# Chunk-by-chunk products ahead of each norm, a third weight pair and a divided gate chain in a two-block transformer on one core

## The chip, the cores and the metric

The kernel runs on one core of a Trainium2 chip. The metric is the device time of one execution in microseconds, the median of several runs. Three runs of the kernel before took 2664.5, 2668.2 and 2671.23 us.

## What is computed

The reference is a transformer of two blocks on one sequence of 512 tokens of width 1024. The first block has two layers over the tokens and, in layer 0, over 256 context tokens beside them. A layer takes a norm with a shift and a scale from a modulation vector, a wide projection, a mixer (a bidirectional chunkwise mLSTM with gates, a gated unit and a convolution over 31 tokens), an out-projection, a second norm, and a gated FFN of 22 x 128 hidden columns. The second block runs two attentions (A: three groups of dilated windows; B: one window of 128 with shared keys), each with a layer norm and a gate behind it:

```
mod = silu(c) @ w_mod[l] + b_mod[l]           # six vectors: sh1, sc1, g1, sh2, sc2, g2
p = (rmsnorm(x, norm1_g) * (1 + sc1) + sh1) @ w_in
x = x + g1 * (mixer(p) @ w_out)
x = x + g2 * swiglu(rmsnorm(x, norm2_g) * (1 + sc2) + sh2, w_gu, w_down)
# second block, twice
x = layer_norm(ALPHA * x + mixer_i(x))
x = x + sigmoid(x @ ple_w_gate[i]) * (p[i] @ ple_w_proj[i])
```

## The kernel before, in words

Every float32 factor is split into a high and a low part, and a product is three matmuls: high by high, low by high, high by low (`mm`, L138). Activations stand in transposed tiles (`Hh`, `Hl`); tokens go in chunks of 128, `c`: six in layer 0, four in layer 1 and in the second block.

Weights come block by block through `wblock` (L154): two loads of 512 KB into `raw` (three buffers, all issued on SP), then for each half a copy to `hi` on ACT and a subtraction to `lo` on DVE. The pool `wp` has two `hi`/`lo` pairs, so a third block's copies wait until TensorE is done with the first. SP issues its loads in their order: a load that waits for a buffer holds back all behind it.

`wide` (L215) makes the 1024 output columns of a product in two halves `n` of 512; for each it takes the two halves `kh` of the inner dimension in turn, and for each `kh` all chunks. It serves the FFN's down products, the products behind both attentions (`post_attention`) and their gate (`embed_gate`).

The FFN of a layer takes its 22 hidden blocks in groups (`GROUPS`: 8, 8 and 6). For each block it multiplies with `w_gu` and leaves the gated result in `ah` and `al`; behind a group the down products add its share to the residual `xt`: `resid` multiplies with the gate `g2` on DVE (`ot`) and adds on POOL (`w`). Behind the last group each chunk is normed (squares on ACT, a sum and a power on DVE and POOL, two scalings) and, by way of the list `pend`, transposed on TensorE (`finish_T`, L338, or `split_T`, L401) for the next stage. `pend.upto(c)` and `pend.keep(n)` say where in the program these transposes stand.

The modulation vectors are made by generators `mod_gen`: one vector takes four steps, in each a load of 1 MB (two of eight row blocks) into `wm` (one buffer) and its matmuls into the bank `md`, which the sixteen records `md<-wm,cact` in the trace are, and a last step that adds the bias and hands the row on. In layer 0's FFN five vectors are made, 20 loads; in layer 1's one, 4 loads. `modl.pump(n)` takes `n` steps behind each hidden block (3 in layer 0, 1 in layer 1), and `modl.drain()` at the end of the first group takes what is left.

`gates` (L641) makes the mLSTM's decay factors in one chain over all engines, which ends in an activation on ACT and six transposes on TensorE (L738). It stands ahead of the convolution's products.

In attention A, heads go in four quads, in each three groups. A quad's first group copies rotated queries and keys (`qh`, `qr`) to `kh`, `qs`, `ks` and `w`, and values to `vb`, by many small DMAs on SP. The tile framework orders each engine's instructions from the program ahead of time; each engine then runs them in that order.

Of the kernel before, what the change touches and what calls it, by code (L numbers as in the profile page):

```python
# [23 lines left out]
GROUPS = [list(range(0, 8)), list(range(8, 16)), list(range(16, 22))]  # L24
# [46 lines left out]
def emit(ctx, tc, a, out):  # L71
    nc = tc.nc
# [81 lines left out]
    def wblock(src, nk, n, into=None):  # L154
        hi, lo = into or (T(wp, [128, nk, n], t, F32R) for t in ("hi", "lo"))
# [49 lines left out]

    def tmj(lhs, wb, n0, n, ps):
# [8 lines left out]
    def wide(src, nk, lhs, chs, bank, use, pre=None, early=None, first=None):  # L215

        for n in range(2):
            ps = {}
            for kh in range(2):
                hi, lo = ({(0, 0): first, (0, 1): early}.get((n, kh)) or wblock(src[n, kh], nk, 512))  # L220
                for c in chs:
                    if pre:
                        pre(c, n, kh)
                    if kh == 0:
                        ps[c] = bank(c)
                    for k in range(nk):
                        lh, ll = lhs(c, nk * kh + k)
                        mm(ps[c], lh, hi[:, k, :], kh + k == 0, False)
                        mm(ps[c], lh, lo[:, k, :], False, False)
                        mm(ps[c], ll, hi[:, k, :], False, kh == 1 and k == nk - 1)  # L230
                    if kh == 1:
                        use(c, n, ps[c])
# [203 lines left out]
    def projections(l, MIX, H, hook):  # L436
# [41 lines left out]
        gates(l, gt, r, t3)  # L478

        for m in range(2):  # L480
            wb = win(4 + m)
# [3 lines left out]
            hook(1)  # L485
            y = yb[:, m, :]
            for p, (o, n) in zip(fm(wb, 128, H, segs), segs):
                stt(y[:, o:o + n], p, col(C_CA + m), sg[:, o:o + n], ADD, MUL)
            convl.add(conv(m, y, yc[:, m, :], col, last, PJ))
# [151 lines left out]
    def gates(l, gt, r, t3):  # L641
# [7 lines left out]
        ax = T(sm, sh, "ga", bufs=1)  # L649
        act(ax, f, AF.Abs)  # L650
        u = T(sm, sh, "gu", bufs=1)
        act(u, ax, AF.Exp, scale=-1.0)
        w = T(sm, sh, "gw", bufs=1)
        ts(w, u, 1.0, ADD)
        lw = T(sm, sh, "glw", bufs=1)
        act(lw, w, AF.Ln)
        rw = T(sm, sh, "grw", bufs=1)
# [9 lines left out]
        for j in range(6):  # L667
            for d, c in enumerate((FCH[j], BCH[j])):
                G.tensor_copy(gpl[:, j, d, 32 * d:32 * d + 4], lf[:, c, d, :])
                G.tensor_copy(gpi[:, j, d, 32 * d:32 * d + 4], gv[:, c, d, 0, :])  # L670
        pc = trt()
# [1172 lines left out]
```

## Time and profile before

| what | value |
|---|---|
| median of three runs | 2668.2 us (2664.5 to 2671.23) |
| profiled execution | 2671.3 us |
| its span | 2669.2 us |
| TensorE busy | 2578.8 us, 97% |
| mean granted TensorE clock | 0.989 |
| DMA | 314.72 MB, mean 118 GB/s |

The span is the time from the first to the last instruction of the profiled execution; the 2.1 us beside it lie around it. TensorE is busy nearly throughout; what it is not busy for lies in short stretches between stages.

### The profile page before, as it was taken

Reading aid. Unit: us, or ns where it says so; the run is one execution under the profiler, and the core shown is the slowest. Engines: PE = TensorE matmul, PEld = TensorE weight load, DVE = VectorE, ACT = ScalarE, POOL = GpSimd, SP = SyncE. Lnnn points to the kernel's source line nnn. Section 1 sums busy time; section 2 is a strip of 40 time slices with the busy share of each in tenths; the row PEclk is TensorE's granted clock in tenths of the full one; section 3 lists DMA queues with packets and bytes.
Section 4 is the critical chain, followed back from the end, with each engine's and each line's share of the span. In section 5 each row is a group of like instructions: output and inputs, shape, how many; then the busy total and the mean of one; then the engine's idle time right before and its main releaser. Section 6 shows DMA issues by size and latency. Waiting matters only on the chain.

```text
span 2669.2 us, 39682 instructions
## 1 busy us (share of the span) xinstructions
PE 2578.8 (97%) x15360; PEld 2166.1 (81%) x15360; DVE 1310.8 (49%) x2802; ACT 964.3 (36%) x2017; POOL 519.9 (19%) x574
## 2 busy tenths in 40 slices
PE   7999999999999998999999999999999999999998
PEld 5888788778888888887878888788787888778787
DVE  5675655223323335766533333534454444675666
ACT  3423535111221225345422222334344344443753
POOL 1155532002002013034302020411111111021102
PEclk9999999999999999999999999999999999999999
DMA  8311553652112123127433232433434344534442
GB/s 301 123 56 46 180 180 112 213 178 64 64 64 64 60 69 106 65 77 223 137 124 95 95 95 83 133 106 98 137 106 130 116 120 125 161 103 141 120 166 79
DMA packets 129979, 314.72 MB, mean 118 GB/s; under 512 B 18528, under 2 KB 48832, under 8 KB 129792
## 3 DMA queue, kind: packets, MB, share of 16 engines
q1 hardware_dynamic: 129792, 312.20, 36.8%
q8 instruction: 121, 1.98, 0.3%
q14 instruction: 66, 0.54, 0.1%
HBM read 272.02 MB, written 13.89 MB: 107 GB/s over the span
## 4 chain that ended last, share of the span: by engine, by line
PE 79%; DVE 7%; DMA 5%; ACT 3%; POOL 3%; issue 2%; SPq 1%; POOLq 0%; DVEq 0%; ACTq 0%
PE mm L138 67%; PE md L138 5%; PE tr L138 5%; PE tr L1228 1%; DVE lo L124 1%; DVE w L124 1%; SPq L1376 1%; POOL w L124 1%; DMA wm<-in_w_mod_dram 1%; DMA t<-mwd 1%; ACT hi L121 1%; DMA raw<-in_a_in_dram 1%; POOL rs L124 1%; ACT t L121 1%; DVE xs L131 1%
## 5 line engine op out<-in xcount | busy, mean ns | idle before, releaser
L138 PE MATMUL mm<-Hh,hi 128*128 128x512 f32 (+1 forms) x2192 | 797.0, 364 | 6.6 <-ACT hi L121 5.5
L138 PE MATMUL mm<-Hl,hi 128*128 128x512 f32 (+1 forms) x2192 | 768.5, 361 | 0.2 <-DVE Hl L124 0.2
L138 PE MATMUL mm<-Hh,lo 128*128 128x512 f32 (+1 forms) x2192 | 712.1, 362 | 0.0
L121 ACT ACTIVATE hi<-raw 128x1024 fp32r<-128x1024 f32 (+2 forms) x334 | 338.0, 1042 | 836.6 <-PE mm L138 461.6
L124 DVE TENSOR_TENSOR lo<-raw,hi 128x1024 fp32r<-128x1024 f32 (+2 forms) x334 | 422.3, 1286 | 299.2 <-ACT hi L121 298.8
L138 PEld LDWEIGHTS mm<-Hh,hi 128*128 128x128 f32 x2192 | 413.8, 189 | 101.4 <-ACT hi L121 8.1
L138 PEld LDWEIGHTS mm<-Hl,hi 128*128 128x128 f32 x2192 | 413.8, 189 | 66.7 <-issue 0.6
L138 PEld LDWEIGHTS mm<-Hh,lo 128*128 128x128 f32 x2192 | 378.3, 189 | 46.9 <-issue 3.5
L124 POOL TENSOR_TENSOR w<-w,ot 128x256 f32<-128x256 f32 x160 | 127.4, 815 | 909.4 <-DVE ot L124 905.2
L124 DVE TENSOR_TENSOR sg<-mm,sg 128x512 f32<-128x512 f32 (+1 forms) x132 | 75.7, 599 | 406.1 <-PE mm L138 233.2
L138 PE MATMUL mm<-hi,Hh 128*128 128x256 f32 (+2 forms) x740 | 225.7, 306 | 6.5 <-ACT Hh L121 3.3
L138 PE MATMUL mm<-hi,Hl 128*128 128x256 f32 (+2 forms) x740 | 221.5, 300 | 0.5 <-POOL Hl L124 0.5
L138 PE MATMUL mm<-lo,Hh 128*128 128x256 f32 (+2 forms) x740 | 220.8, 299 | 0.0
L124 POOL TENSOR_TENSOR qr<-rt,rt 128x512 f32<-128x512 f32 x58 | 85.5, 1487 | 487.0 <-DVE rt L124 366.9
L138 PEld LDWEIGHTS mm<-hi,Hh 128*128 128x128 f32 x740 | 141.6, 192 | 15.3 <-ACT Hh L121 3.7
L138 PEld LDWEIGHTS mm<-hi,Hl 128*128 128x128 f32 x740 | 141.9, 192 | 6.1 <-issue 1.2
L138 PEld LDWEIGHTS mm<-lo,Hh 128*128 128x128 f32 x740 | 142.2, 192 | 3.7
L138 PE MATMUL mm<-hi,ah 128*128 128x512 f32 x352 | 139.3, 396 | 0.0
L138 PE MATMUL mm<-hi,al 128*128 128x512 f32 x352 | 139.2, 396 | 0.0
L138 PE MATMUL mm<-lo,ah 128*128 128x512 f32 x352 | 139.2, 396 | 0.0
L138 PE MATMUL mm<-hi,Yh 128*128 128x256 f32 (+1 forms) x416 | 130.3, 313 | 5.2 <-DVE t L124 3.1
L124 DVE TENSOR_TENSOR rt<-mm,cs 128x512 f32<-128x512 f32 x116 | 75.5, 685 | 116.6 <-PE mm L138 111.7
(369 smaller groups left out, 3692.8 us busy)
## 6 DMA issues: line engine op xcount, KB each, us to landing
raw<-in_w_gu_dram SPq DMA_DIRECT2D x88, 512.0 KB
raw<-in_a_in_dram SPq DMA_DIRECT2D x72, 512.0 KB
wm<-in_w_mod_dram SPq DMA_DIRECT2D x24, 1024.0 KB
raw<-in_w_in_dram SPq DMA_DIRECT2D x40, 512.0 KB
raw<-in_w_d_dram SPq DMA_DIRECT2D x40, 512.0 KB
raw<-in_w_mod_dram SPq DMA_DIRECT2D x36, 512.0 KB
t<-mwd SPq DMA_DIRECT2D x38, 256.0 KB
raw<-in_w_out_dram SPq DMA_DIRECT2D x16, 512.0 KB
```

The lines of the kernel that those rows point to most:

```text
L121: return S.activation(o, i, f, **kw)
L124: return (e or V).tensor_tensor(out=o, in0=x, in1=y, op=op)
L131: (e or V).tensor_scalar(out=o, in0=x, scalar1=s1, scalar2=None, op0=op0)
L138: lasts["P"] = PE.matmul(o, lhsT=l, rhs=r, start=start, stop=stop, **kw).ins
L1228: PE.transpose(pt[:, 128 * i:128 * i + 128], e, ident)
L1376: ld(d["v"][32 * c:32 * c + 32, b, :], d["vr"][32 * b:32 * b + 32, c, :])
```

## The change

- `GROUPS` becomes 4, 6, 6 and 6 hidden blocks; `ah` and `al` have six buffers in place of eight; the down weights are packed to fit.
- `wblock` has three `hi`/`lo` pairs. The gates' temporaries move into one tile of the convolution's pool, and the DMA scratch is set to 512.
- `wide` loads both `kh` halves of its second half `n` and takes it chunk by chunk (both `kh` for a chunk before the next): in the last FFN group, behind attention and in the gate. The out-projection takes its last two column blocks chunk by chunk.
- `w_gu[0]` (in layer 1 `w_gu[1]` too) is loaded during the out-projection. In layer 1 a new function, `fm_pairs`, takes the first 256 tokens of the first two FFN blocks before the others.
- `gates` becomes a generator whose steps stand between the convolution's products.
- The points at which chunks are transposed move: `pend.keep(1)` in layer 0's last group too, `upto(c + 1)` in `embed_gate`, `upto(1 + j)` at attention A's first products.

```diff
@@ -21,7 +21,7 @@
...
 HID = 22
-GROUPS = [list(range(0, 8)), list(range(8, 16)), list(range(16, 22))]
+GROUPS = [list(range(0, 4)), list(range(4, 10)), list(range(10, 16)), list(range(16, 22))]
 FCH = [4, 5, 0, 1, 2, 3]
@@ -152,7 +152,7 @@
     def wblock(src, nk, n, into=None):
-        hi, lo = into or (T(wp, [128, nk, n], t, F32R) for t in ("hi", "lo"))
+        hi, lo = into or (T(wp, [128, nk, n], t, F32R, bufs=3) for t in ("hi", "lo"))
         h = (nk + 1) // 2
@@ -203,6 +203,16 @@
...
+    def fm_pairs(wbs, H, first):
+        pss = [[[mmt()] for _ in range(2)] for _ in wbs]
+        for q in range(2):
+            for i, wb in enumerate(wbs):
+                pend.upto(first + i if q == 0 else 9)
+                for m in range(2):
+                    fm_into([pss[i][m][0][:, 256 * q:256 * q + 256]], wb, 128 * m, H, [(256 * q, 256)])
+        return pss
     def tmj(lhs, wb, n0, n, ps):
@@ -212,24 +222,30 @@
...
-    def wide(src, nk, lhs, chs, bank, use, pre=None, early=None, first=None):
+    def wide(src, nk, lhs, chs, bank, use, pre=None, early=None, first=None, by_chunk=True):
         for n in range(2):
-            ps = {}
-            for kh in range(2):
-                hi, lo = ({(0, 0): first, (0, 1): early}.get((n, kh)) or wblock(src[n, kh], nk, 512))
-                for c in chs:
-                    if pre:
-                        pre(c, n, kh)
-                    if kh == 0:
-                        ps[c] = bank(c)
-                    for k in range(nk):
-                        lh, ll = lhs(c, nk * kh + k)
-                        mm(ps[c], lh, hi[:, k, :], kh + k == 0, False)
-                        mm(ps[c], lh, lo[:, k, :], False, False)
-                        mm(ps[c], ll, hi[:, k, :], False, kh == 1 and k == nk - 1)
-                    if kh == 1:
-                        use(c, n, ps[c])
+            ps, wb = {}, {}
+            order = [(kh, c) for kh in range(2) for c in chs]
+            if n and by_chunk:
+                wb = {kh: wblock(src[n, kh], nk, 512) for kh in range(2)}
+                order = [(kh, c) for c in chs for kh in range(2)]
+            for kh, c in order:
+                if kh not in wb:
+                    wb[kh] = {(0, 0): first, (0, 1): early}.get((n, kh)) or wblock(src[n, kh], nk, 512)
+                hi, lo = wb[kh]
+                if pre:
+                    pre(c, n, kh)
+                if kh == 0:
+                    ps[c] = bank(c)
+                for k in range(nk):
+                    lh, ll = lhs(c, nk * kh + k)
+                    mm(ps[c], lh, hi[:, k, :], kh + k == 0, False)
+                    mm(ps[c], lh, lo[:, k, :], False, False)
+                    mm(ps[c], ll, hi[:, k, :], False, kh == 1 and k == nk - 1)
+                if kh == 1:
+                    use(c, n, ps[c])
@@ -475,17 +491,22 @@
...
         qT = T(MIX, [128, 4, TT_], "qT")
-        gates(l, gt, r, t3)
-
+        gsteps = gates(l, gt, r, t3, PJ)
+        next(gsteps)
+        wbc = [win(4), win(5)]
         for m in range(2):
-            wb = win(4 + m)
+            wb = wbc[m]
             sg = t3()
...
             hook(1)
+            next(gsteps, None)
             y = yb[:, m, :]
...
                 stt(y[:, o:o + n], p, col(C_CA + m), sg[:, o:o + n], ADD, MUL)
+            if m == 0:
+                next(gsteps)
             convl.add(conv(m, y, yc[:, m, :], col, last, PJ))
@@ -646,15 +667,20 @@
...
         sh = [128, 6, 2, 4]
-        ax = T(sm, sh, "ga", bufs=1)
+        sp = T(PJ, [128, 256], "ct", bufs=1)
+        def small(i):
+            return sp[:, 48 * i:48 * i + 48].rearrange("p (c d h) -> p c d h", c=6, d=2)
+        ax = small(0)
         act(ax, f, AF.Abs)
-        u = T(sm, sh, "gu", bufs=1)
+        u = small(1)
         act(u, ax, AF.Exp, scale=-1.0)
-        w = T(sm, sh, "gw", bufs=1)
+        w = small(2)
         ts(w, u, 1.0, ADD)
-        lw = T(sm, sh, "glw", bufs=1)
+        lw = small(3)
         act(lw, w, AF.Ln)
-        rw = T(sm, sh, "grw", bufs=1)
+        rw = small(4)
         V.reciprocal(out=rw, in_=w)
@@ -668,6 +694,7 @@
...
                 G.tensor_copy(gpi[:, j, d, 32 * d:32 * d + 4], gv[:, c, d, 0, :])
+        yield
         pc = trt()
@@ -708,6 +735,7 @@
...
                     tt(mp[p, j + 1:j + 2], br[p, j, le:le + 1], M[p, j, le:le + 1], ADD)
+        yield
         for d in range(2):
@@ -733,6 +761,7 @@
...
         act(E, E, AF.Exp, scale=-1.0)
+        yield
         pe_ = trt()
@@ -949,11 +978,17 @@
...
         rest = [c for c in chs if c >= ne]
-        for n, cc in ((0, first), (1, first), (0, rest), (1, rest), (2, chs), (3, chs)):
-            if n not in wbo:
-                wbo[n] = wblock(a["w_out"][l, n], 8, 256)
-            wb = wbo[n]
-            for c in cc:
+        gu = {}
+        order = [(n, c) for n, cc in ((0, first), (1, first), (0, rest), (1, rest)) for c in cc]
+        order += [(n, c) for c in chs for n in (2, 3)]
+        for n, c in order:
+                if n not in wbo:
+                    wbo[n] = wblock(a["w_out"][l, n], 8, 256)
+                if (n, c) == (3, chs[-2]):
+                    gu[0] = wblock(a["w_gu"][l, 0], 8, 256)
+                if last and (n, c) == (3, chs[-1]):
+                    gu[1] = wblock(a["w_gu"][l, 1], 8, 256)
+                wb = wbo[n]
                 if n or c >= ne:
@@ -978,12 +1013,20 @@
...
             for jj in grp:
-                with behind("AV" if jj == 1 else ""):
-                    wb = wblock(a["w_gu"][l, jj], 8, 256)
-                ah = T(FP, [128, TT_], "ah", F32R, bufs=8)
-                al = T(FP, [128, TT_], "al", F32R, bufs=8)
-                if jj == 0:
+                if jj in gu:
+                    wb = gu[jj]
+                else:
+                    with behind("AV" if jj == 1 else ""):
+                        wb = wblock(a["w_gu"][l, jj], 8, 256)
+                ah = T(FP, [128, TT_], "ah", F32R, bufs=6)
+                al = T(FP, [128, TT_], "al", F32R, bufs=6)
+                if jj == 0 and last:
+                    both = fm_pairs([wb, gu[1]], H2, 2)
+                    pg, pu = both[0]
+                elif jj == 0:
                     pg, pu = fm_pair(wb, H2, segs)
+                elif jj == 1 and last:
+                    pg, pu = both[1]
                 else:
@@ -1015,7 +1058,7 @@
...
                 if lastg and n2 == 1:
-                    pend.keep(1 if last else 2)
+                    pend.keep(1)
                 for n in (2 * n2, 2 * n2 + 1):
@@ -1025,9 +1068,9 @@
...
-            wide(a["w_d8"][l, gi] if gi < 2 else a["w_d6"][l], len(grp) // 2,
+            wide(a["w_d4"][l] if gi == 0 else a["w_d6"][l, gi - 1], len(grp) // 2,
                  lambda c, k: [t[:, 128 * c:128 * c + 128] for t in acts[grp[k]]], chs,
-                 lambda c: mmt() if c < 4 else (mdt, trt)[c - 4](), down)
+                 lambda c: mmt() if c < 4 else (mdt, trt)[c - 4](), down, by_chunk=lastg)
         close(FP)
@@ -1293,7 +1336,7 @@
...
         def pre(c, n, kh):
-            pend.upto(c + 2)
+            pend.upto(c + 1)
             if (n, kh) == (0, 1):
@@ -1384,7 +1427,7 @@
...
                 for j, (i, m) in enumerate(((0, 0), (0, 1), (1, 0))):
-                    pend.upto(3 if h or j else 2)
+                    pend.upto(3 if h else 1 + j)
                     half = lambda z: from_residue(z)[:, 2 * h:2 * h + 2]
@@ -1830,7 +1874,7 @@
...
-    nc = bacc.Bacc("TRN2", target_bir_lowering=False, num_devices=1)
+    nc = bacc.Bacc("TRN2", target_bir_lowering=False, num_devices=1, dynamic_dma_scratch_size=512)
     arrays, args = {}, {}
```

What moves, first on TensorE in layer 0's FFN, at the last modulation pieces (`md<-wm,cact`, one row for a piece; `mm<-hi,ah` and the like are down products). Before, the last piece of all and its surroundings:

```order
L138 MATMUL mm_5952<-hi_5903,ah_4999 128x512
L138 MATMUL mm_5952<-lo_5904,ah_4999 128x512
L138 MATMUL mm_5952<-hi_5903,al_5000 128x512
L138 MATMUL mm_5952<-hi_5903,ah_5150 128x512
L138 MATMUL md_5718<-wm_5873,cact 32x256 x8
L138 MATMUL mm_5952<-lo_5904,ah_5150 128x512
L138 MATMUL mm_5952<-hi_5903,al_5151 128x512
L138 MATMUL mm_5913<-hi_5991,ah_5300 128x512
```

The change, from the twelfth of the twenty pieces on:

```order
L138 MATMUL mm_5580<-hi_5549,al_4593 128x512
L138 MATMUL md_5253<-wm_5296,cact 32x256 x8
L138 MATMUL mm_5580<-hi_5549,ah_4846 128x512
L138 MATMUL mm_5580<-lo_5550,ah_4846 128x512
L138 MATMUL mm_5580<-hi_5549,al_4847 128x512
L299 MATMUL tr_5308<-ident,mb_5254 128x128 x2
L138 MATMUL md_5312<-wm_5315,cact 32x256 x8
L138 MATMUL md_5312<-wm_5325,cact 32x256 x8
L138 MATMUL md_5312<-wm_5335,cact 32x256 x8
L138 MATMUL md_5312<-wm_5345,cact 32x256 x8
L138 MATMUL md_5360<-wm_5364,cact 32x256 x8
L138 MATMUL md_5360<-wm_5374,cact 32x256 x8
```

Before, at least 23 products lie ahead of every piece; in the change the last eight pieces stand in a row, two more of them behind the last row shown, and three products and two transposes ahead of them.

Next on TensorE in layer 1, where the gates' chain ends (`tr<-ident,w` are the six transposes; `mm_9603`, `mm_9645`, and in the change `mm_9690`, `mm_9747` and `mm_9792` are the convolution's inputs). Before:

```order
L138 MATMUL mm_9603<-Hh_8425,lo_9567 128x512
L138 MATMUL mm_9645<-Hh_8425,hi_9634 128x512
L138 MATMUL mm_9645<-Hl_8426,hi_9634 128x512
L738 MATMUL tr_9552<-ident,w_9549 128x36 x6
L138 MATMUL mm_9645<-Hh_8425,lo_9635 128x512
L138 MATMUL mm_9645<-Hh_8425,hi_9634 128x512
L138 MATMUL mm_9645<-Hl_8426,hi_9634 128x512
```

The change:

```order
L138 MATMUL mm_9747<-Hh_8545,lo_9583 128x512
L138 MATMUL mm_9747<-Hh_8545,hi_9582 128x512
L138 MATMUL mm_9747<-Hl_8546,hi_9582 128x512
L138 MATMUL mm_9747<-Hh_8545,lo_9583 128x512
L767 MATMUL tr_9778<-ident,w_9738 128x36 x6
L138 MATMUL mm_9792<-Hh_8545,hi_9582 128x512
L138 MATMUL mm_9792<-Hl_8546,hi_9582 128x512
L138 MATMUL mm_9792<-Hh_8545,lo_9583 128x512
```

Before, the transposes stand behind two matmuls of the second product; in the change behind all 24 of it.

Last on SP at the first boundary between quads of attention A (`raw` are weights, `kh`, `qs` and `ks` the copies of the quad's first group). Before:

```order
L159 DMA raw_16041<-in_a_in_dram 128x1024
L159 DMA raw_16045<-in_a_in_dram 128x1024
L159 DMA raw_16231<-in_a_in_dram 128x1024
L1171 DMA kh_15837<-qh_15848 32x512 x8
L1171 DMA qs_15835<-qr_15846 32x512 x4
L1171 DMA ks_15836<-qr_15846 32x512 x4
L1171 DMA kh_15837<-qh_15869 32x512 x8
L1171 DMA qs_15835<-qr_15867 32x512 x4
L1171 DMA ks_15836<-qr_15867 32x512 x4
```

The change:

```order
L159 DMA raw_16305<-in_a_in_dram 128x1024
L159 DMA raw_16491<-in_a_in_dram 128x1024
L159 DMA raw_16495<-in_a_in_dram 128x1024
L159 DMA raw_16651<-in_a_in_dram 128x1024
L1214 DMA kh_16097<-qh_16108 32x512 x8
L1214 DMA qs_16095<-qr_16106 32x512 x4
L1214 DMA ks_16096<-qr_16106 32x512 x4
```

Before, one half (`raw_16231`) of the blocks that follow the first group stands ahead of the copies (the two loads ahead of it are the values' weights), and the next half behind the sixteen `vb` copies; in the change three stand ahead (from `raw_16491` on), and the fourth behind `vb` and the next block's `qs` copies.

## Rows read from the trace of the kernel before

**Rows 1.** The page's busy time by engine.

```profile
PE 2578.8 (97%) x15360; PEld 2166.1 (81%) x15360; DVE 1310.8 (49%) x2802; ACT 964.3 (36%) x2017; POOL 519.9 (19%) x574
```

**Rows 2.** Stretches: width, PE busy (instructions), granted clock, DMA share, GB/s.

```profile
440.00:600.00 160.00, 159.19 (x1092) 1.00 0.57 196
110.00:126.00 16.00, 14.09 (x76) 0.89 0.03 6
996.00:1030.00 34.00, 25.30 (x151) 0.95 0.50 164
1070.00:1090.00 20.00, 16.18 (x65) 0.83 0.18 57
1300.00:1320.00 20.00, 16.16 (x121) 0.91 0.17 58
1680.00:1716.00 36.00, 29.92 (x177) 0.91 0.43 147
1876.00:1900.00 24.00, 19.38 (x122) 0.93 0.47 141
2016.00:2040.00 24.00, 19.01 (x125) 1.00 0.44 137
2156.00:2180.00 24.00, 20.16 (x125) 0.93 0.46 137
2306.00:2390.00 84.00, 80.26 (x352) 0.98 0.38 120
2608.00:2648.00 40.00, 37.24 (x170) 0.96 0.11 36
```

**Rows 3.** Waits, 1070 to 1090: engine, line, releaser; us, times, longest.

```profile
PE tr L738 <- ACT w L121: 3.8, 1, 3.8
```

**Rows 4.** Waits of PE in layer 0's FFN, 440 to 600.

```profile
PE md L138 <- DMA wm<-in_w_mod_dram: 0.6, 3, 0.2
```

**Rows 5.** The chain that ended last, layer 0's FFN: start, us, what.

```profile
485.18 5.30 DMA wm<-in_w_mod_dram
...
490.52 1.07 PE md L138 x16
491.59 5.55 PE mm L138 x31
```

**Rows 6.** The same chain, a run of down products.

```profile
620.85 11.24 PE mm L138 x48
```

**Rows 7.** Waits of PE at the first quad boundary, 1876 to 1900.

```profile
PE mm L138 <- ACT hi L121: 2.2, 1, 2.2
PE tr L1228 <- ACT sb L121: 1.0, 2, 0.8
```

**Rows 8.** Timeline of SP ahead of that boundary: start, us, what was issued.

```profile
1831.12 1.76 SPq L159 DMA_DIRECT2D raw<-in_a_in_dram  x2
1843.76 4.97 SPq L1171 DMA_DIRECT2D kh<-qh  x8
...
1877.94 10.05 SPq L1376 DMA_DIRECT2D vb<-vr  x16
1888.04 11.14 SPq L159 DMA_DIRECT2D raw<-in_a_in_dram  x6
```

**Rows 9.** Timeline at the end of layer 1's FFN, one chunk's norm chain.

```profile
1684.34 0.76 DVE L124 TENSOR_TENSOR ot<-mm,g 128x256 f32<-128x256 f32 x2 [6.77 <-PE mm L138]
...
1689.13 0.66 PE L401 MATMUL tr<-ident,w 128*128 128x128 f32 x4 [0.70 <-DVE w L127]
...
1690.26 0.66 PE L401 MATMUL tr<-ident,w 128*128 128x128 f32 x4 [0.47 <-POOL w L124]
```

**Rows 10.** The page's groups of instructions: the residual adds on POOL.

```profile
L124 POOL TENSOR_TENSOR w<-w,ot 128x256 f32<-128x256 f32 x160 | 127.4, 815 | 909.4 <-DVE ot L124 905.2
```

**Rows 11.** The page's DMA queues: packets, MB, share of 16 engines.

```profile
q1 hardware_dynamic: 129792, 312.20, 36.8%
```

More of the change, by code (lines that the diff above doesn't have):

```diff
@@ L639, in conv_post, with gates @@
                 tt(o, o, sg[:, 256 * m:256 * m + 256], MUL, e=G)
-    def gates(l, gt, r, t3):
+    def gates(l, gt, r, t3, PJ):
         gpl = t3(432).rearrange("p (j d e) -> p j d e", j=6, d=2)
@@ L1797, in n2 @@
         return np.stack([np.stack([_blk(w[h * k:h * k + h], _rng(512 * n, 512)) for k in range(2)]) for n in range(2)])
-    a["w_d8"] = np.stack([np.stack([n2(f["w_down"][l][1024 * g:1024 * g + 1024]) for g in range(2)]) for l in range(2)])
-    a["w_d6"] = np.stack([n2(f["w_down"][l][2048:]) for l in range(2)])
+    a["w_d4"] = np.stack([n2(f["w_down"][l][:512]) for l in range(2)])
+    a["w_d6"] = np.stack([np.stack([n2(f["w_down"][l][768 * g + 512:768 * g + 1280]) for g in range(3)])
+                          for l in range(2)])
     a["final_g"] = f["final_g"]
```

## The prediction

> **What bounds the kernel now.** I read the page's busy shares first. TensorE is busy for 2578.8 of 2669.2 us, 97% [rows 1]; DVE, ACT and POOL stand at 49%, 36% and 19% on the page. So the change can win nothing by taking work from another engine. It can win only the time in which TensorE stands still or runs at the lower of its two clocks (a granted clock of 0.5 is 1.2 GHz, 1.0 is 2.4 GHz), and it must not open new holes. So the second view was the table of stretches, where width less PE busy is idle time and one less the granted clock, times the width, is at most what the low clock cost [rows 2]. Ten of its stretches are the boundaries that the diff touches:
>
> - the gates of layer 0 (110 to 126): 1.9 idle and 1.8 of clock; of layer 1 (1070 to 1090): 3.8 and 3.4
> - end of layer 0's FFN (996 to 1030): 8.7 and 1.7; of layer 1's (1680 to 1716): 6.1 and 3.2
> - layer 1's out-projection to its FFN (1300 to 1320): 3.8 and 1.8
> - the three boundaries between quads of heads in attention A (1876, 2016, 2156): 4.6, 5.0, 3.8 idle, 1.7, 0.0, 1.7 of clock
> - the products behind attention A and B (2306 to 2390, 2608 to 2648): 3.7 and 1.7, 2.8 and 1.6
>
> These add up to 62.8 us: all that the parts on waits can earn. The eleventh stretch, 440 to 600 in layer 0's FFN, has 0.8 us idle in 160 and a full clock. There a new hole costs its whole length.
>
> **The change part by part.** *Gate chain.* In layer 1 TensorE waits 3.8 us for the chain that ends in an activation on ACT [rows 3], with two matmuls ahead of it; now 24 stand there. One matmul of 512 columns takes 0.234 us (48 in 11.24) [rows 6], so the 22 more are 5.1 us, longer than the wait. I take 6.5 of the 7.2 there and 3.5 of the 3.7 in layer 0, where 48 products stand ahead of it.
>
> *Products by chunk.* With both halves of the weights at hand, one chunk's sums are done while the next chunk's products still run, so its residual add, norm and transposes lie beside products. At the end of layer 0's FFN a chunk takes 36 matmuls in the last half, 8.4 us, and the last two transposes come behind projections of the next layer: 8.5 of 10.4. In layer 1's out-projection the first halves of two FFN blocks now stand between the last product and the last transposes: 4.5 of 5.6. At the end of layer 1's FFN little stands behind the last product, and the last chunk's chain shows its length: its first sum leaves PSUM at 1684.34, TensorE starts on the two halves of that chunk at 1689.13 and 1690.26 [rows 9], 4.8 and 5.9 us later. What is late next is this chain, so I take 2.5 of 9.3. Behind attention the products by chunk and the later transposes of the gate leave half a chain: 7 of 9.8.
>
> *Third weight pair.* At the first quad boundary TensorE waits 2.2 us for `hi`, the weights, and 1.0 for `sb`, the scores [rows 7]. The cause stands on SP: the loads of the next blocks are issued at 1888.04, behind the copies for the first group that begin at 1843.76 and the sixteen `vb` copies of 1877.94 [rows 8], because one half block was all that found room ahead of them. Now three halves stand ahead, a whole block and a half; a whole block is 48 matmuls, 11.2 us, against 4.6 us idle. But the fourth half now stands on SP behind the `qs` copies of the block that was brought forward, so a rest of the wait for weights can stay: 14 of 16.8 for the three.
>
> *New FFN groups.* 4, 6, 6, 6 in place of 8, 8, 6 adds a pass of the down products: 40 more adds of 0.815 us on POOL [rows 10], 33 us on an engine busy for a fifth of the span, and as many products on DVE; TensorE's matmuls stay the same. Cover: the FFN's matmuls; cost taken as nothing. The smaller DMA scratch and the moved temporaries are taken as nothing too: all loads went over the hardware queue [rows 11].
>
> *What the new groups do to the modulation loads.* This is the large negative term. Layer 0's FFN also computes 20 pieces of 1 MB of modulation weights through one buffer, `wm`. Three steps go out per hidden block, and what is left at the end of the first group is drained at once. With eight blocks nearly all 25 steps lay among products: TensorE waited 0.6 us for these loads, three times [rows 4]. With four blocks twelve steps do, and the rest comes behind the fourth block. By the order on TensorE two of the drained pieces still lie among down products, and the last eight stand in a row with nothing between them. With one buffer a load can't start until the piece before it is multiplied. One such round is read from the chain: load issued at 485.18, 5.30 us, its sixteen matmul records 1.07, the next product at 491.59 [rows 5], 6.41 us. Of that TensorE works 1.07, which was there before too; 5.34 is now idle. Eight rounds are 42.7; the three products behind the piece before them take 0.7 off: **42**.
>
> To it comes the clock. Nine of the ten boundary stretches show a granted clock under 1 [rows 2]. If all eight pieces run at the low level, their 1.07 us double: 0 to 8.6, and I take 4, between the ends. The first products after it lose another 1.7 (as at the quad boundaries), and the last add on DVE some 0.5. **The drain costs 48, with ends at 42 and 53.** The Trainium skill (TensorE: Matmul & The Clock Gate, section HAM oscillation — how this bites in real kernels) describes a kernel whose groups of matmuls wait for loads and fall back to the low clock time after time; by it the upper end would hold and the forecast would be 5 us higher. The rows above speak neither way on pieces this short.
>
> Layer 1's FFN has only four pieces for its four blocks, 23 to 48 matmuls apart, at least 5.4 us beside a load of 5.3: 0 to 2, taken as nothing.
>
> **The sum.** Gains: 3.5 + 6.5 + 8.5 + 4.5 + 2.5 + 14 + 7 = 46.5. Cost 48. Net +1.5 against the profiled execution: 2671.3 + 1.5 = 2672.8. That execution lies 3.1 above the median of the three runs (2668.2), so in terms of the median 2669.7; rounded, **2669 us**. It is a forecast of two large terms that cancel.
>
> **The rivals.**
> 1. *All the waits go, and the drain is short.* For it: with more products at hand each boundary has more cover than its wait is long, and without a hole the clock stays up. Against it: layer 1's FFN end has no cover. 62.8 gained, 42 paid: 21 faster, 2647. Chance 0.28, taken with the ground between it and the forecast, from about 2660 down.
> 2. *The last chunk's norm chain stays the bound* (slower). By chunk the chain of every chunk but the last is covered; the last is as long as before, 4.8 to 5.9 us [rows 9]. It decides wherever fewer than some 25 matmuls of 512 columns stand between the last product and its transposes. If that holds at the end of both FFNs, in the out-projection and behind attention, each of the five keeps 5 us and the clock that goes with it. Their gains of 22.5 fall to about 9, and the drain at 48 to 53 stands: 46.5 − 13.5 = 33 against 48 to 53, 15 to 20 slower, 2683 to 2688. Chance 0.24.
> 3. *The drain does not stall.* The change would not do to the loads what the order says if the transfers were done by the time that TensorE comes to them. Against it: one buffer, and 5.3 us a piece even where the 16 DMA engines were half idle (0.57 in that stretch [rows 2]). Then only the gains are left: 2621. Chance 0.05.
>
> **How the numbers follow.** The forecast holds 0.43, rival 1 0.28, rival 2 0.24, rival 3 0.05. A measurement of this kernel can tell about 0.3%, 8 us, from no change. The forecast's own spread, about 8 us to each side, lies mostly within that; part of rival 1 lies within it too, and a little of the forecast outside. Faster 0.32, same 0.42, slower 0.26. The range reaches from rival 1's time to rival 2's upper end with 2 us for what I took as nothing, 2647 to 2690; rival 3 lies below it, and some 0.12 is left out on both sides beyond that.
>
> **What would show it right or wrong.** In the profile after, eight groups of sixteen `md` records in layer 0's FFN should stand about 6.4 us apart with nothing between them, and the wait of `md` for `wm` should be over 40 us instead of 0.6. SP should issue three halves of `raw` ahead of the `kh` copies at each quad boundary, and the wait for `hi` there should be under 1 us. The wait for the gates' activation should be gone in both layers; the end of layer 1's FFN should still show a hole of 3 us or more. The prediction is wrong if the drain's wait is under 35 us, or if the ten boundaries give back less than 30 or more than 60 us.

## The result

The change is slower by 0.9%: 2693.35 us, the median of four runs (2685.58 to 2694.78), against 2668.35 us for four runs of the kernel before (the three above and one more). The ratio is 1.0089, with a 95% interval of 1.0066 to 1.0112. The forecast was 2669 with a range of 2647 to 2690; the measured time lies 3 us above the range, on the side of rival 2.

The profiled execution took 2693.03 us, 21.7 more than that of the kernel before. The page's busy line, against [rows 1]:

```profile
PE 2570.1 (95%) x15408; PEld 2168.1 (81%) x15408; DVE 1330.6 (49%) x2858; ACT 971.6 (36%) x2034; POOL 574.2 (21%) x614
```

TensorE's busy time is 8.7 us less and its span 22.1 longer: it stands idle for 31 us more. Where, the table of stretches shows (width, PE busy and instructions, granted clock, DMA share, GB/s). These are the stretches of [rows 2] at their places in the profile after, the one behind attention A 6 us wider, in the same order:

```profile
434.00:594.00 160.00, 112.76 (x760) 0.82 0.51 170
118.00:134.00 16.00, 16.00 (x95) 1.00 0.13 39
1041.00:1075.00 34.00, 31.52 (x210) 1.00 0.42 148
1111.00:1131.00 20.00, 20.00 (x98) 1.00 0.20 58
1328.00:1348.00 20.00, 14.98 (x99) 0.75 0.33 108
1708.00:1744.00 36.00, 31.62 (x189) 0.91 0.40 139
1916.00:1940.00 24.00, 22.26 (x158) 0.93 0.54 163
2052.00:2076.00 24.00, 22.26 (x171) 1.00 0.55 165
2186.00:2210.00 24.00, 22.25 (x159) 0.93 0.52 157
2320.00:2410.00 90.00, 82.29 (x358) 0.96 0.43 134
2632.00:2672.00 40.00, 35.97 (x154) 0.96 0.17 54
```

The first row is the modulation loads in layer 0's FFN: 0.8 us idle became 47.2, and the mean granted clock fell to 0.82. TensorE is busy throughout both gates and at full clock now, and the end of layer 0's FFN is idle for 2.5 us instead of 8.7. The quad boundaries went from 4 or 5 us idle to 1.7 each. But the out-projection of layer 1 (fifth row) is worse, 5.0 idle instead of 3.8 and a clock of 0.75, and so are both stretches behind attention: 7.7 and 4.0 instead of 3.7 and 2.8.

A second reading gives the price of each place. The same piece of work is looked up in the timeline of both profiles; how much later it starts than before, less how much later the piece ahead of it started, is what the stretch between them lost (+) or won (−). The pieces are the first and last product of both out-projections, the last down product of both FFNs, the first value product of attention A, the first product behind it, the first score of attention B and the last matmul. Steps against the kernel before, in us, from one profiled execution of each kernel:

| kernel | to out-proj. 0 | out-proj. 0 | FFN 0 | FFN 0 end to out-proj. 1 | out-proj. 1 | FFN 1 | to attention A | A with its boundaries | behind A | B and behind | sum |
|---|---|---|---|---|---|---|---|---|---|---|---|
| the change | −6.4 | 1.9 | 49.3 | −15.5 | −1.5 | 0.8 | −0.9 | −14.0 | 6.3 | 1.3 | 21.2 |
| e1 | −4.9 | 0.2 | −1.6 | −16.3 | −0.8 | 0.7 | −1.0 | −14.9 | 6.9 | 1.3 | −30.4 |
| e2 | 0.8 | −1.4 | 58.4 | 0.4 | −0.4 | 0.3 | 1.6 | 2.7 | −1.6 | 0.0 | 60.9 |
| e3 | −6.5 | 3.9 | 48.2 | −14.6 | −0.4 | 0.4 | −1.2 | −13.9 | 1.6 | 0.5 | 18.1 |
| e4 | −0.8 | 2.6 | 1.4 | −10.2 | 0.0 | −0.7 | 0.6 | −15.4 | −1.4 | −0.7 | −24.7 |
| e5 | −7.6 | 3.6 | −3.0 | −14.6 | −1.4 | 0.1 | −1.4 | −13.7 | −0.3 | 0.5 | −37.8 |
| e6 | −7.2 | 0.4 | −2.5 | −15.6 | −1.2 | 1.1 | −0.8 | −14.0 | 6.7 | −0.2 | −33.5 |
| e7 | −5.5 | 3.7 | 1.0 | −14.4 | −2.1 | −0.2 | −1.5 | −13.5 | −0.3 | 0.6 | −32.2 |
| e8 | −5.4 | 2.3 | −3.7 | −15.3 | −1.2 | 3.8 | −0.3 | −14.0 | −0.2 | 0.6 | −33.4 |
| e9 | −7.4 | 0.3 | −3.0 | −14.6 | −0.5 | 0.8 | −1.1 | −12.9 | −1.3 | −0.7 | −40.4 |
| e10 | −7.1 | 3.8 | 5.4 | −15.3 | 0.1 | 0.0 | −1.0 | −15.1 | 5.3 | −0.2 | −24.2 |
| e11 | −7.6 | 3.6 | −2.3 | −15.2 | 1.2 | −2.8 | −0.2 | −13.9 | 0.8 | −0.6 | −37.0 |
| e12 | −5.0 | 5.4 | −4.1 | −16.1 | 0.3 | −6.2 | −1.2 | −13.4 | −1.4 | −0.6 | −42.4 |

A step of a few us can be the clock alone. Layer 0's out-projection has the same order of matmuls in e9 and in e12, and yet their steps differ by 5.1 us. Its stretch in e9, then in e12:

```profile
311.00:416.00 105.00, 96.02 (x816) 0.98 0.50 166
313.50:423.50 110.00, 100.14 (x817) 0.94 0.48 159
```

The idle time is 9.0 and 9.9 us; the rest of the difference goes with the granted clock, 0.98 against 0.94. Why it was lower is not known. So a single step below some 5 us shows little. The steps behind attention A repeat: +5.3 to +6.9 in the four kernels whose gate goes by chunk (the change, e1, e6, e10), −1.6 to +1.6 in the nine others.

The hole in layer 0's FFN is the round trip that the forecast worked out. First the wait of TensorE, 430 to 600 (us, times, longest), then its timeline in the drain (start, us, what, idle before and releaser), then the clock of the whole drain:

```profile
PE md L138 <- DMA wm<-in_w_mod_dram: 46.3, 13, 5.6
```

```profile
523.29 1.07 PE L138 MATMUL md<-wm,cact 128*32 128x256 f32 x16
...
529.89 1.94 PE L138 MATMUL md<-wm,cact 128*32 128x256 f32 x16 [4.09 <-DMA wm<-in_w_mod_dram]
536.91 1.93 PE L138 MATMUL md<-wm,cact 128*32 128x256 f32 x16 [5.08 <-DMA wm<-in_w_mod_dram]
544.15 1.93 PE L138 MATMUL md<-wm,cact 128*32 128x256 f32 x16 [5.30 <-DMA wm<-in_w_mod_dram]
```

```profile
529.00:587.00 58.00, 19.10 (x138) 0.50 0.41 135
```

The piece at 523.29 still takes 1.07 us, as in [rows 5]; from the next on a piece takes 1.93, at a granted clock of 0.5, which is 1.2 GHz, and the next piece starts 7.0 to 7.5 us later. All eight ran at the low clock, and so did the products up to 587. The eight waits sum to 41.5 us; the other 4.7 lie at earlier pieces. The Trainium skill (TensorE: Matmul & The Clock Gate, section HAM oscillation — how this bites in real kernels) describes groups of matmuls that wait for loads and fall back to the low clock; the trace agrees, with the granted clock at 0.50 throughout.

### The profile page after: what moved, and what is told of

Its sections match the earlier page's. It is cut to its first block, busy times and chain, and to the rows that moved or that the text cites. A ratio compares the mean times of both kernels' runs of the same rounds, so it can differ in the third digit from the quotient of the medians.

```text
span 2691.3 us, 39898 instructions
## 1 busy us (share of the span) xinstructions
PE 2570.1 (95%) x15408; PEld 2168.1 (81%) x15408; DVE 1330.6 (49%) x2858; ACT 971.6 (36%) x2034; POOL 574.2 (21%) x614
## 4 chain that ended last, share of the span: by engine, by line
PE 84%; DMA 5%; DVE 4%; ACT 3%; POOL 2%; issue 2%; SPq 0%; DVEq 0%; POOLq 0%; ACTq 0%
PE mm L138 70%; PE md L138 6%; PE tr L138 5%; DMA wm<-in_w_mod_dram 3%; PE tr L1271 1%; POOL w L124 1%; DMA t<-mwd 1%; ACT t L121 1%; DVE lo L124 1%; DVE t L124 1%; ACT hi L121 0%; DVE w L124 0%; DMA g<-gd 0%; POOL t L124 0%; ACT sb L121 0%
## 5 line engine op out<-in xcount | busy, mean ns | idle before, releaser
L121 ACT ACTIVATE hi<-raw 128x1024 fp32r<-128x1024 f32 (+1 forms) x350 | 341.3, 1003 | 826.6 <-PE mm L138 373.1
L124 DVE TENSOR_TENSOR lo<-raw,hi 128x1024 fp32r<-128x1024 f32 (+1 forms) x350 | 426.6, 1232 | 271.0 <-ACT hi L121 270.6
L124 POOL TENSOR_TENSOR w<-w,ot 128x256 f32<-128x256 f32 x200 | 171.4, 881 | 893.8 <-DVE ot L124 891.6
L138 PE MATMUL mm<-hi,Yl 128*128 128x256 f32 (+1 forms) x416 | 129.0, 310 | 1.5 <-POOL Yl L124 1.5
```

Of the source, the lines that this page charges most:

```text
L121: return S.activation(o, i, f, **kw)
L124: return (e or V).tensor_tensor(out=o, in0=x, in1=y, op=op)
L138: lasts["P"] = PE.matmul(o, lhsT=l, rhs=r, start=start, stop=stop, **kw).ins
```

## The experiments

Each kernel is the change, or the kernel before, with the edit shown. Ratios are to runs of the kernel before that were taken beside each kernel (medians of 2667.55 to 2669.47 us).

### e1: the modulation loads over two FFN groups

```diff
-                modl.pump(1 if last else 3)
+                modl.pump(1 if last else 3 + (0 < jj < 4) if jj < 4 else 2)
...
-            if gi == 0:
+            if gi == (0 if last else 1):
                 modl.drain()
                 close(MP)
```

> The change as it is, but layer 0's twenty modulation loads are spread over the first two FFN groups: 15 of the 25 steps over the four blocks of the first group, two behind each block of the second, so that no two pieces stand in a row. Groups of 4, 6, 6, 6 and everything else stay. Theory (the drain is the loss): TensorE's wait for these loads falls from over 45 us to under 3, the stretch from the last out-projection to layer 0's last down product falls by 47 to 50 us, and the time by as much, 2693 to about 2645. Rival (the smaller groups themselves cost, by one more pass of residual adds): half or more of the 49 us stays, 2665 or above.

Measured: 2641.17 us, ratio to the kernel before 0.9902 (0.9887 to 0.9917). The wait in this FFN, 430 to 720:

```profile
PE md L138 <- DMA wm<-in_w_mod_dram: 3.2, 5, 1.3
```

The FFN's step went from +49.3 to −1.6, and the time fell by 52 us, as the theory had it. The four groups with their added pass cost nothing that can be seen; the drain was all of the FFN's loss.

### e2: the groups alone

```diff
-GROUPS = [list(range(0, 8)), list(range(8, 16)), list(range(16, 22))]
+GROUPS = [list(range(0, 4)), list(range(4, 10)), list(range(10, 16)), list(range(16, 22))]
```

(in the kernel before, with the down weights packed to fit)

> The kernel before with the one edit of the groups, 4, 6, 6, 6 in place of 8, 8, 6 (two weight pairs, products and gates as before). Theory (the drain comes with the groups alone): eight modulation pieces stand in a row again, TensorE runs them at the low clock, and the time rises by 47 to 53 us, 2668 to 2715 to 2721. Rival (the loss needs the third weight pair, which brings products forward and leaves none for the drain): the rise is under 35 us, below 2703.

Measured: 2726.47 us, ratio 1.022 (1.0202 to 1.0237). The waits in 430 to 720:

```profile
PE md L138 <- DMA wm<-in_w_mod_dram: 47.9, 12, 5.6
```

The drain comes with the groups and needs nothing else of the change. The time rose by 59 us, more than the theory's 47 to 53; the FFN lost 58.4, 9.1 more than in the change. One more round is most of it: only two products lie ahead of the twelfth piece (23 in the change), so that nine pieces are multiplied with next to nothing between them, and a round at the low clock takes 7.2 to 7.5 us. So the rival falls: the loss does not need the third pair. Which of the change's other edits makes the drain shorter there was not tested by itself.

### e10: two buffers for the loads

```diff
-            wm = (T(pool, [128, 2, 1024], "wm", bufs=1) if pool
+            wm = (T(pool, [128, 2, 1024], "wm", bufs=2) if pool
```

> The change as it is, with two buffers for the modulation loads instead of one; the eight pieces still stand in a row. Theory (the round trip through one buffer is the cost): the next load is under way while a piece is multiplied, a round falls from 7.3 us to the 3 to 4 us that the transfer needs, and the time by 24 to 34, to 2660 to 2669. Rival (the transfer itself takes the 5.3 us): a round stays at 5 us or more and the time falls by less than 18, 2675 or above.

Measured: 2649.82 us (two runs), ratio 0.9928 (0.9901 to 0.9956): 43.5 less than the change, more than the theory asked for. The waits for `wm` in 430 to 560, the last pieces, and the stretch that they stand in:

```profile
PE md L138 <- DMA wm<-in_w_mod_dram: 6.8, 4, 2.8
```

```profile
527.19 1.07 PE L138 MATMUL md<-wm,cact 128*32 128x256 f32 x16 [0.70 <-DMA wm<-in_w_mod_dram]
530.41 1.07 PE L138 MATMUL md<-wm,cact 128*32 128x256 f32 x16 [2.15 <-DMA wm<-in_w_mod_dram]
534.26 1.94 PE L138 MATMUL md<-wm,cact 128*32 128x256 f32 x16 [2.78 <-DMA wm<-in_w_mod_dram]
537.37 1.93 PE L138 MATMUL md<-wm,cact 128*32 128x256 f32 x16 [1.17 <-DMA wm<-in_w_mod_dram]
```

```profile
527.00:538.00 11.00, 4.71 (x56) 0.71 0.99 373
```

Where TensorE waits for the loads, a round is 3.1 to 3.9 us, as the theory has it; only the last two pieces ran at the low clock. Each load still takes 5.2 to 6.0 us from its issue to its piece, but two are under way at a time, and the DMA engines are busy for 0.99 of the stretch, against 0.41 in the drain of the change. The gain is larger than the shorter round alone, because the order changed as well: with two buffers, most of the pieces were set among down products, and the last three alone stood in a row. So this run shows that loads can follow each other faster than one in 5.3 us. It doesn't show what two buffers would be worth with the pieces still in a row; that was not tried.

### e4: the third weight pair alone

```diff
-        hi, lo = into or (T(wp, [128, nk, n], t, F32R) for t in ("hi", "lo"))
+        hi, lo = into or (T(wp, [128, nk, n], t, F32R, bufs=3) for t in ("hi", "lo"))
```

(in the kernel before, with the gates' temporaries moved and the small DMA scratch, to make room)

> The kernel before with a third weight pair and nothing else of the change but what makes room for it (the gates' temporaries in a tile of the convolution's pool, the small DMA scratch). Theory (the pair works at the quad boundaries of attention A and hardly elsewhere): three halves of raw stand ahead of the kh copies, each boundary gives 4 to 5 us, 12 to 15 in all, 2668 to 2653 to 2656. Rivals: the boundaries' gain needs the rest of the change, 2664 or above; or the pair feeds the ends of FFN and out-projection too, 2648 or below.

Measured: 2646.65 us, ratio 0.9923 (0.9909 to 0.9938), 21 us less, outside the theory on the side of the second rival. The boundaries gave 15.4, as expected; another 10.2 came between the end of layer 0's FFN and layer 1's out-projection. There the pair does most of what the forecast put down to products by chunk. Not all of it: ahead of the last down product TensorE waits 2.6 us for ACT's reads of transposed rows (`tr L338 <- ACT t`), before and in e4 alike, and in the change that wait is gone. The waits around the first boundary, 1840 to 1960, against [rows 7]:

```profile
PE tr L1454 <- ACT sb L121: 0.7, 1, 0.7
PE mm L138 <- ACT hi L121: 0.5, 1, 0.5
PE mm L138 <- DVE lo L124: 0.5, 1, 0.5
```

These are the same three waits, to the tenth, as in the change. The boundaries' gain needs nothing but the pair and the room made for it; the moved temporaries and the small scratch were not run without the pair.

### e3, e6, e7: the gate behind attention

All three undo parts of the gate's edit: e3 both parts, in the change; e6 and e7 one part each, in the kernel of e1. The two parts are

```diff
-            pend.upto(c + 1)
+            pend.upto(c + 2)
...
-        wide(a["ple_g"][i], 4, ..., range(4), bank4, use, pre, early)
+        wide(a["ple_g"][i], 4, ..., range(4), bank4, use, pre, early, by_chunk=False)
```

> The change, with the gate behind attention as in the kernel before: its second half not chunk by chunk, and the transposes ahead of it two chunks ahead instead of one. The products of the out-projections behind attention stay chunk by chunk. Theory (the gate is what turned the expected 7 us of gain behind attention into 7.7 of loss): the two stretches fall by 8 to 14 us, the time from 2693 to 2679 to 2685. Rival (the loss lies in the out-projection's second half chunk by chunk, whose last norm comes late): less than 4 us come back, 2689 or above.

> As the change with the modulation loads spread (2641), and of the gate one half alone as before: its transposes two chunks ahead of the product again; its second half stays chunk by chunk. Read by stretch from the profile. Theory (both halves of the gate's edit cost): the waits of 0.8, 1.1 and 1.8 us for transposes and for the activations copied behind them go, 2 to 4 us less behind attention A and 1 to 2 less behind B; the hole of 3.7 us ahead of attention B stays. Rival: the waits only move to the next product, under 1 us in each.

> The other half alone, on the same kernel: the gate's second half not chunk by chunk, its transposes late as in the change. Theory: the hole of 3.7 us ahead of attention B goes with the low clock behind it, 4 to 6 us less behind attention A, and nothing changes behind B, where no transposes follow the gate. Rival (the hole is owed to the late transposes): it stays, and less than 1 us comes back.

Measured: e3 2685.4 us (ratio to before 1.0067, 1.0051 to 1.0083), 8 less than the change by the medians, 3.9 by the profiled executions; behind A +6.3 became +1.6, behind B 1.3 became 0.5. Those 5.5 us lie between the theory's 8 to 14 and the rival's 4. The parts were run once each: e6 2637.41 us, e7 2638.73, where e1 has 2641.17; they are read by the steps of the table. Behind A, e6 leaves 6.7 of e1's 6.9 and e7 leaves −0.3, 7.2 us less. Waits of TensorE behind A, before (2300 to 2400):

```profile
PE tr L338 <- DVE w L133: 2.3, 1, 2.3
PE mm L138 <- DVE o L124: 0.9, 1, 0.9
```

in the change (2320 to 2425):

```profile
PE tr L397 <- DVE w L124: 3.7, 1, 3.7
PE md L138 <- ACT Hh L121: 1.8, 1, 1.8
PE mm L138 <- ACT Hh L121: 1.1, 2, 0.8
PE tr L354 <- DVE w L133: 1.1, 1, 1.1
```

in e6 (2280 to 2365):

```profile
PE tr L397 <- DVE w L124: 5.4, 1, 5.4
PE tr L354 <- DVE w L133: 1.8, 1, 1.8
PE md L138 <- ACT Hh L121: 1.6, 1, 1.6
PE mm L138 <- ACT Hh L121: 0.8, 1, 0.8
```

and in e7 (2280 to 2365):

```profile
PE md L138 <- ACT Hh L121: 1.8, 1, 1.8
PE mm L138 <- ACT Hh L121: 1.1, 2, 0.8
PE tr L354 <- DVE w L133: 1.1, 1, 1.1
PE mm L138 <- ACT pg L121: 0.8, 1, 0.8
```

The wait `tr L397` is for the rows that the gate itself has just finished (`w`, by an add on DVE), which are transposed for attention B. Going by chunk, the first chunk's products end after 24 of 96; its transposes come some five products later, while DVE still works off the gate's first half. Taking the half for all chunks gives them time, and the wait is gone, and with it the low clock: over the stretch behind A the granted clock is 0.97 in e1 and 1.00 in e7. With the earlier transposes alone (e6) that wait grows, 3.7 to 5.4. So behind A e7's theory held, with a little more than it asked for, and for e6 the rival was right. Behind B e6 is 1.5 us better and e7 0.7, but no wait went there: the waits around the gate sum to 4.3 us in e6 and 4.5 in e7, against 4.0 in the change. What differs is the granted clock over the stretch, 1.00 in e6 and e7 and 0.99 in e1; e10, whose gate is the change's, stands 1.5 better too. So e6's theory fell in both places.

### e5: both repairs

> The change with both repairs: modulation loads spread over two FFN groups, and the gate behind attention as in the kernel before. Theory (the two losses are separate): the 8 us of the old gate add to the spread loads, 2641 to 2630 to 2636, faster than either kernel. Rival (the old gate helps only where the clock is disturbed by what comes before): 2638 or above.

Measured: 2634.26 us, ratio 0.9877 (0.9854 to 0.99), as the theory had it. The two losses are separate, and their repairs add: 6.9 less than e1.

### e9, e11: without going by chunk at all

e9 takes e5 and passes `by_chunk=False` in `post_attention` too; e11 takes e9 and orders the out-projections' last two column blocks as before the change.

> As the kernel with both repairs, and the out-projections behind attention not chunk by chunk either. Theory (there the last chunk's norm chain sets the end, and going by chunk brings nothing): within 3 us of the kernel with both repairs. Rival (going by chunk brings the forecast 5 us and more, and only the gate gave it back): 5 us or more above it.

> As the kernel without chunks behind attention, and the out-projections of the mixers, too, take a column block for all chunks at a time, as before the change; the early loads and the pairs of FFN blocks stay. Theory (the hole behind layer 1's out-projection comes from the transposes of two chunks in a row, which wait for PSUM banks that ACT has to empty, whichever order the products have): within 2 us. Rival (by chunk gains in the out-projection what was forecast): 4 us or more slower.

Measured: e9 2631.08 us, 3.2 less than e5, ratio 0.9861 (0.9836 to 0.9886); e11 2631.85 us, ratio 0.9862 (0.9847 to 0.9877). Going by chunk behind attention brought nothing: undone, the two stretches are 1.0 and 1.2 us better, no more than the clock can do, and the rest of the difference between e9 and e5 lies where the two kernels have the same code. TensorE's wait for the normed rows of the second block did get shorter by chunk. Behind A (2260 to 2355) it is in e9, then in e5:

```profile
PE tr L354 <- DVE w L133: 2.9, 2, 2.3
PE tr L354 <- DVE w L133: 1.8, 1, 1.8
```

but the stretch as a whole did not. In layer 1's out-projection and FFN together (the two columns), e11 stands 1.9 us better than e9. Nothing was won by chunk there either; in layer 0, e11's 3.6 lies among the 0.2 to 5.4 of kernels that all go by chunk there. Only the last FFN groups still go by chunk in e11; that was not undone.

### e8, e12: the transposes behind layer 1's out-projection

```diff
-                    both = fm_pairs([wb, gu[1]], H2, 2)
+                    both = fm_pairs([wb, gu[1]], H2, 1)
```

(e8, in the kernel of e5)

```diff
-                if n == 3:
+                if n == (2 if last else 3):
                     pend.keep(1)
```

(e12, in the kernel of e9)

> As the kernel with both repairs, and in layer 1's first two FFN blocks the third chunk's transposes stand behind the first block's first products instead of ahead of all. Theory: TensorE's wait of 3.8 us for the third chunk's scaled rows, right behind the out-projection, goes, and the low clock behind it with it: 4 to 7 us less than with both repairs alone. Rival (the last chunk's chain is the bound there and the wait only moves on): less than 2 us.

> As the kernel without chunks behind attention, and in layer 1's out-projection a chunk is transposed one column block earlier, so that the second chunk's transposes stand 24 products ahead of the end and the third's alone behind it. Theory (16 transposes in a row need four PSUM banks and there are three, so that they wait for ACT): the waits of 3.8 and 1.3 us there go, and of the low clock behind them 1 us or more: 4 to 7 us less than without the edit, about 2625. Rival (the third chunk's own chain ends no sooner): the wait stays with the third chunk, less than 2 us less.

In the change TensorE waits behind the last product of that out-projection like this (1328 to 1348):

```profile
PE tr L354 <- ACT t L121: 3.8, 1, 3.8
PE mm L138 <- DVE rv L131: 1.3, 1, 1.3
```

The releaser `t` is ACT's read of transposed rows out of PSUM, not the rows to be transposed: sixteen transposes of the second and third chunk stand in a row, four to a bank, and three banks hold twelve. Twelve are done at 1336.0; ACT comes to the first bank only behind two copies of weights, and TensorE goes on at 1339.77:

```profile
1336.34 1.99 ACT L121 ACTIVATE hi<-raw 128x1024 fp32r<-128x1024 f32 x2
1338.23 1.48 ACT L121 ACTIVATE t<-tr,modc,modc 128x128 f32<-128x128 f32 x4
```

So half of the wait is the copies' place in ACT's order; no run moved them. e8 measured 2639.46 us (ratio 0.9891, 0.9872 to 0.991), 5 us above e5. Its theory fell. The framework's order left the sixteen where they were and moved the fourth chunk's transposes from behind 50 products to behind 96; the 3.7 us stayed, and a new wait of 1.9 us for the fourth chunk's activations came on top. e12 does part them: the second chunk's stand 24 products ahead of the end. It measured 2627.93 us, ratio 0.9843 (0.9827 to 0.9858), the lowest median here, though its interval overlaps those of e9 and e11. Its waits in the same place (1260 to 1305):

```profile
PE tr L354 <- ACT t L121: 1.6, 1, 1.6
PE mm L138 <- DVE ot L124: 0.9, 1, 0.9
```

and the stretch 1281 to 1301 with its clock:

```profile
1281.00:1301.00 20.00, 17.84 (x150) 1.00 0.32 107
```

Out-projection and FFN of layer 1 together are 6.2 us better than in e9, as the theory had it; idle time in the FFN fell by 3.6, and the rest goes with the clock. The time as a whole fell by only 3, under the theory's 4 to 7. In the profiled executions it fell by 2, since the same code in layer 0's out-projection took 5.1 us longer in e12, at the lower clock shown above.

## Why the prediction was wrong

**The drain was right.** It was forecast at 48 us, with ends at 42 and 53; the FFN lost 49.3. The eight waits sum to 41.5 (forecast 42). All eight pieces ran at 1.2 GHz, 6.9 us where 4 had been taken, so the rounds came every 7.0 to 7.5 us and not every 6.4.

**Three of the gains were right in size.** The quad boundaries gave 14.0 (forecast 14). From the end of layer 0's FFN to layer 1's out-projection 15.5 came (8.5 and 6.5). Up to layer 0's out-projection it was 6.4 (3.5 for the gates), of which 1.9 went again behind it. One of them was right in part by luck. At the end of layer 0's FFN and the start of layer 1, 10.2 of the 15.5 come with the third pair alone (e4), without the order by chunk. The working there misread the kernel as well: a chunk takes 18 matmuls in the last half, 4.2 us, and not 36 and 8.4.

**The step that failed** is "behind attention the products by chunk and the later transposes of the gate leave half a chain: 7 of 9.8". It was 7.6 lost instead (6.3 and 1.3), 14.6 us on one term. Two things were missed. First, the order by chunk wins nothing in the products behind attention (e9): the wait for the last normed rows gets shorter, the stretch does not. What takes its place was not followed up. Rival 2 had said that little would be won there, and the forecast still booked a gain. Second, the same order in the gate brings the first chunk's end forward by many products, and with it the transposes that wait for it, ahead of the work that DVE still has (e7): 7.2 us. The forecast looked at what the order does to the last chunk and never at the first.

**The smaller misses**: layer 1's out-projection to FFN, 4.5 forecast, 0.7 by the two columns. Before, TensorE waited there for the scaled rows of the norm chain (1300 to 1320):

```profile
PE tr L338 <- DVE xs L131: 2.6, 2, 2.3
```

In the change that wait is gone, and the one for the banks of the transposes, which ACT empties late, has taken its place (e12). And 0.9 came for 2.5 at the end of layer 1's FFN. Its waits after, 1708 to 1744, show the chain of the last chunk that the forecast named, and a wait for weights behind it:

```profile
PE tr L417 <- POOL w L124: 2.5, 2, 1.3
PE mm L138 <- ACT hi L121: 1.7, 1, 1.7
```

Together these misses are 14.6 + 3.8 + 1.6 = 20.0 us; the forecast's net was +1.5, the steps measured 21.2. The forecast had named a sign of its being wrong, that the boundaries give back less than 30 us. By the steps they gave back 28, where 46.5 was forecast.

Rival 2 came nearest in time, 5 us short of the measured one. Its places were right in four of five: out-projection, end of layer 1's FFN and both stretches behind attention, but not the end of layer 0's FFN. Its mechanism, the last chunk's norm chain, is seen at the end of layer 1's FFN alone; in the out-projection it was the banks, and behind attention 7.2 us are the first chunk's.

## What to carry to other kernels

Before a loop is cut into smaller groups, list what is pumped along by its iterations: work that was hidden by the count of steps is drained in the open when the count falls, and through one buffer each piece costs the whole round trip (5.3 us of load beside 1.07 of work here, and half a clock on top). An order by chunk shortens the wait for the last chunk, if anything; look also at who waits for the first chunk, which now ends earlier while the engines behind it are still busy. And an edit to an order is worth a run by itself: a third weight pair gave 21 us alone, while the orders by chunk that were undone here had given nothing or taken some back. When two kernels differ by a few us, look at where, and at the granted clock there, before an edit gets the credit.

## What was not expected of the hardware

- One 1 MB load at a time took 5.0 to 5.5 us from issue to piece in the drain. For the one issued at 546.14 the packets ran from 547.17 to 551.00, and its piece started at 551.33: 1.0 us ahead of the transfer, 3.8 of transfer, 0.3 behind it. With two outstanding (e10), a piece came every 3.1 to 3.9 us with the DMA engines busy for 0.99 of the time.
- The same code in layer 0's out-projection took between 104.5 us (e1) and 109.6 us (e12) in the profiled executions, first to last product. The order of matmuls is the same in both, and the idle time differs by under 1 us; the granted clock was 0.98 and 0.94.
